# A fused diffusion step: the first norm with features on the partitions instead of transposing x on the chip

## The chip, the cores and the metric

The kernel runs on one core of one Trainium2 chip. The metric is the device time of one execution in microseconds (us). The kernel before takes 1057.17 us, the median of three runs (1056.76 to 1060.57).

## The reference, cut to what matters

One trunk layer works on 640 tokens of width 1024: 512 latent tokens and 128 context tokens. The change lies in its first step, the norm with modulation ahead of the big input projection:

```
h = rmsnorm(x, pre1) * (1 + scale1) + shift1        # shift1, scale1: from silu(c) @ w_ada + b_ada
mq, mk, mv, mo, mg, cq, ckv, krope, merge = split(h @ w_in)
```

rmsnorm divides each token by the root of the mean of its 1024 squares; scale and shift have one value per feature, and differ between latent and context tokens. After this come a bidirectional mLSTM, an attention, a merge and an MLP of width 4096, which the change does not touch.

## The kernel before, in words

Activations that feed a projection are kept with the features on the 128 partitions: h1h and h1l, 8 blocks of 128 features by 640 tokens, are the high and the low part of h, and every product is three float32r matmuls (high by high, high by low, low by high).

The head of the kernel (L175 to L232) makes h. x is read as five tiles of 128 tokens by 1024 features (L185 to L188). Per tile ACT squares and sums it along the free axis (L194), `rstd_of` takes the mean on DVE (L98) and the power -1/2 on POOL (L100), and DVE scales the tile by it (L196). Two blocks of the query weights are loaded meanwhile; `load_w` casts them to the high part on ACT (L111) and takes the low part on POOL here (L112).

`features(k)` then works on block k of 128 features. It issues the load of block k+1 of the modulation weights (aw, 1 MB each, L181, six buffers). `ada_rows` multiplies block k of those weights with silu(c) in eight plain float32 matmuls (L149) and copies the sums out (L150). `ada_cols` transposes them (L155) and adds up four partial sums (L157, L158); two small DVE instructions make the factor A and the offset B (L206, L207). Five transposes on TensorE (L210, L211) bring the x block into PSUM with features on the partitions. ACT and DVE each apply A and B (L215 writes h1h, L216 a float32 copy), once for the 512 latent and once for the 128 context tokens, and DVE takes the low part as the difference (L217).

The loop at L222 calls `features(k + 1)` and then issues the twelve query matmuls of block k (L229). Right behind it come the p1 products (L269 onwards), whose weights partly reuse the buffers of the query weights.

The order in which an engine issues its instructions is not that of the source: a planner goes through the program with its own model of times and puts the instructions of each engine in the order in which it finds them ready. All loads of the head are issued from SP's queue.

Of the kernel before, what the change touches and what calls it, by code (L numbers as in the profile page):

```python
# [6 lines left out]
F32 = mybir.dt.float32  # L7
# [19 lines left out]
def _build(ctx, tc, nc, a, dbg):  # L27
# [44 lines left out]
    def bank2():  # L72
        return psum[2][1].tile([P, 1024], F32, name="b2")
# [21 lines left out]
    def rstd_of(ss, n, width, name):  # L95

        ms = small.tile([P, 8], F32, name="ms")[:, 0:n]
        V.tensor_scalar(out=ms, in0=ss, scalar1=1.0 / width, scalar2=EPS, op0=ALU.mult, op1=ALU.add)  # L98
        r = small.tile([P, 8], F32, name="rs_" + name)[:, 0:n]
        G.tensor_tensor(out=r, in0=ms, in1=mhalf[:, 0:n], op=ALU.pow)  # L100
        return r

    def load_w(src, eng=V):

        n = src.shape[1]
        raw = pW_.tile([P, 1024], F32, name="raw", bufs=2)[:, 0:n]
# [23 lines left out]
    def halves(ps):  # L130
        return ps.rearrange("p (h n) -> p h n", h=2)
# [41 lines left out]
        S.activation(out=qT[:, j, :].rearrange("p (h n) -> p h n", h=2), in_=ps[:, :, 0:320], func=AF.Copy, scale=128.0 ** -0.5)  # L173

    with pool("pX", side="right") as pX:  # L175
        xt = []
        aw = []

        def ada_load(f):
            w = pX.tile([P, KD, 256], F32, name="aw", bufs=6)  # L180
            nc.sync.dma_start(w, a["w_ada1"][f].rearrange("p (k n) -> p k n", k=KD))  # L181
            aw.append(w)
        ada_load(0)
        nc.sync.dma_start(cst[:, 0:128], a["consts"][:, 0:128])
        for t in range(NT):  # L185
            x = pX.tile([P, 1024], F32, name=f"x{t}")
            nc.sync.dma_start(x, a["x"][t])
            xt.append(x)  # L188
        wq = [[x.rearrange("p (k n) -> p k n", k=8) for x in load_w(a["w_q"][j], G)] for j in range(2)]
        qps = [halves(bank2()) for j in range(2)]  # L190
        for t in range(NT):
            sq = pX.tile([P, 1024], F32, name="sq", bufs=1)
            ss = small.tile([P, 1], F32, name="ss")
            S.activation(out=sq, in_=xt[t], func=AF.Square, accum_out=ss)  # L194
            r = rstd_of(ss, 1, 1024, "x")
            V.tensor_scalar(out=xt[t], in0=xt[t], scalar1=r, scalar2=None, op0=ALU.mult)  # L196

        def features(k):
            if k + 1 < KD:
                ada_load(k + 1)  # L200
            rows = pX.tile([P, 256], F32, name="ar", bufs=2)
            ada_rows([aw[k][:, i, :] for i in range(KD)], 256, rows)
            pc = bank1()
            m = ada_cols(rows, 2, pc[:, 128:384].rearrange("p (b x) -> p b x", b=2), 2 * k, "1")
            A, B = modA[0][:, k, :], modB[0][:, k, :]
            V.tensor_scalar(out=A, in0=m[:, 0, :], scalar1=1.0, scalar2=pre1[:, k:k + 1], op0=ALU.add, op1=ALU.mult)  # L206
            V.tensor_copy(B, m[:, 1, :])  # L207
            px = bank1()
            for t in range(4):
                T.transpose(px[:, t * 128:(t + 1) * 128], xt[t][:, k * 128:(k + 1) * 128], ident)  # L210
            T.transpose(pc[:, 0:128], xt[4][:, k * 128:(k + 1) * 128], ident)  # L211

            tmp = pX.tile([P, TOK], F32, name="tmp", bufs=3)
            for ps, c, i in ((px, slice(0, 512), 1), (pc[:, 0:128], slice(512, 640), 0)):
                S.activation(out=h1h[:, k, c], in_=ps, func=AF.Identity, scale=A[:, i:i + 1], bias=B[:, i:i + 1])  # L215
                V.tensor_scalar(out=tmp[:, c], in0=ps, scalar1=A[:, i:i + 1], scalar2=B[:, i:i + 1], op0=ALU.mult, op1=ALU.add)  # L216
            V.tensor_tensor(out=h1l[:, k, :], in0=tmp, in1=h1h[:, k, :], op=ALU.subtract)  # L217

        features(0)
        nc.sync.dma_start(cst[:, 128:640], a["consts"][:, 128:640])  # L220
        nc.sync.dma_start(hvec, a["hvec"])
        for k in range(KD):  # L222
            if k + 1 < KD:
                features(k + 1)
            for u, v in ((0, h1h), (1, h1h), (0, h1l)):
                for j in range(2):
                    for hf in range(2):
                        c = slice(hf * 320, hf * 320 + 320)
                        T.matmul(qps[j][:, hf, 0:320], wq[j][u][:, k, :], v[:, k, c], start=k == 0 and u == 0 and v is h1h,  # L229
                                 stop=k == KD - 1 and v is h1l)  # L230
        for j in range(2):
            q_evac(j, qps[j])  # L232
# [933 lines left out]
def prepare(i):  # L1166
    import numpy as np
    c_ = np.ascontiguousarray
    cols = lambda v: c_(v.reshape(-1, 128).T)
    d = {}  # L1170
    d["x"] = c_(np.concatenate([i["x_sample"][0], i["x_prompt"][0]], 0).reshape(5, 128, 1024))
    d["cache_ckv"] = c_(i["cache_mla_ckv"][0, 0])
    d["cache_krope"] = c_(i["cache_mla_krope"][0, 0])
    cn = i["state_mlstm_C"][0, 0].transpose(0, 2, 1, 3)
    nn = i["state_mlstm_n"][0, 0].transpose(0, 2, 1)[..., None]
    d["state"] = c_(np.concatenate([cn, nn], -1))
    cv = np.stack([i["c_ctx"], i["c"][0]], -1)
    cv = cv.reshape(8, 128, 2).transpose(1, 0, 2).reshape(128, 16)
    wa = i["w_ada"][0].reshape(1024, 6, 8, 128)
    d["w_ada1"] = _piece_a(wa[:, [1, 0]].transpose(0, 2, 1, 3).reshape(1024, 2048), 8, 256)  # L1180
    d["w_ada2"] = _piece_a(wa[:, [4, 3, 2, 5]].reshape(1024, 4096), 2, 512)
    b = i["b_ada"][0].reshape(6, 8, 128)
    b = np.concatenate([b[[1, 0]].transpose(1, 0, 2).reshape(16, 128), b[[4, 3, 2, 5]].reshape(32, 128)], 0).reshape(-1)
    d["vecs"] = c_(np.concatenate([cols(i["norm_pre1"][0]), cols(i["norm_pre2"][0]), c_(i["mlstm_head_norm"][0].T), cols(b),
                                   cols(i["norm_post1"][0]), cols(i["norm_post2"][0]), cv], 1))
    gb = i["mlstm_gate_b"][0]
    d["hvec"] = c_(np.stack([gb[:, 0].reshape(8), gb[:, 1].reshape(8), i["state_mlstm_m"][0, 0].reshape(8)], 1))
    d["kv_norm"], d["q_norm"] = c_(i["mla_kv_norm"][0]), c_(i["mla_q_norm"][0])
    w = i["w_in"][0]
    d["w_q"], d["w_k"] = _piece_b(w[:, 0:512]), _piece_b(w[:, 512:1024])  # L1190
    d["w_v"], d["w_o"] = _piece_a(w[:, 1024:1536], 2, 512), _piece_b(w[:, 1536:2048])
    d["w_p1"] = _piece_a(np.concatenate([w[:, 2048:2064], w[:, 2448:2704], w[:, 2704:2736]], 1), 2, 304)
    d["w_cq"] = _piece_a(w[:, 2064:2448], 2, 384)
    d["w_g"] = _piece_b(w[:, 2736:4784])
    d["w_uq"] = _piece_a(i["w_uq"][0].reshape(384, 768), 1, 768)
    ukv = i["w_ukv"][0]
    d["w_uk"] = c_(_piece_b(ukv[:, :, 0:64].reshape(256, 512)).transpose(1, 0, 2).reshape(128, 1024))
    d["w_uv"] = _piece_a(ukv[:, :, 64:128].reshape(256, 512), 2, 512)[0]
    d["w_y"] = c_(np.concatenate([_piece_b(i["w_mlstm_o"][0]), _piece_b(i["w_mla_o"][0])], 2))
    d["w_out"] = _piece_a(i["w_out"][0], 2, 512)  # L1200
    d["w_mlp1"] = _piece_b(i["w_mlp1"][0])
# [45 lines left out]
```

## Time and profile before

| what | value |
|---|---|
| median of three runs | 1057.17 us (1056.76 to 1060.57) |
| the profiled execution, its own time | 1055.42 us |
| its span, first to last instruction | 1053.7 us |
| TensorE (PE) busy | 1022.7 us, 97% of the span |
| VectorE (DVE) busy | 561.0 us |
| ScalarE (ACT) busy | 424.2 us |
| GpSimd (POOL) busy | 238.1 us |
| read from HBM | 105.03 MB |

Busy time is that of one engine's instructions; PE stands for the matmuls and PEld for the loads of their stationary side, which overlap them. The chain that ended last is followed back from the last instruction to what released each one. Times within the span count from its start.

### The profile page before, as it was taken

The page shows a single profiled execution, that of the slowest core. Times are in us where ns is not written, and L with a number is a line of the kernel's source. Part 1 is how long each engine was busy: PE and PEld are TensorE (multiplying, and loading weights), DVE is VectorE, ACT ScalarE, POOL GpSimd, SP SyncE. Part 2 cuts the span into 40 slices and gives each one's busy share as a digit, 9 for nine tenths or more (in the row PEclk, how much of TensorE's full clock was granted, in tenths as well). Part 3 has the DMA queues.
Part 4 walks back from the last instruction along what each step waited for, and adds up shares of the span by engine and source line. Part 5 has one row for each costly group of instructions (what it writes and reads, how often), then busy time and mean ns, then how long its engine had stood idle before and what let it go on. Part 6 is the DMA issues. An engine that isn't in the chain of part 4 may idle for free.

```text
span 1053.7 us, 15728 instructions
## 1 busy us (share of the span) xinstructions
PE 1022.7 (97%) x6342; PEld 907.0 (86%) x6342; DVE 561.0 (53%) x955; ACT 424.2 (40%) x784; POOL 238.1 (23%) x218
## 2 busy tenths in 40 slices
PE   4999999899999999999999998999999999999997
PEld 2899899888889888888888897898989898989896
DVE  4655255767664222222334489365566565656557
ACT  4354244277775222222223564442425152515142
POOL 3011225424560000001000015224040404040101
PEclk9999999999999999999999999999999999999999
DMA  9444132211002444444446251231313131313034
GB/s 372 168 129 145 46 109 73 75 41 41 15 8 79 139 143 140 141 140 141 140 141 223 77 180 62 79 121 40 120 40 120 40 120 41 121 41 121 1 111 169
DMA packets 40121, 112.03 MB, mean 106 GB/s; under 512 B 4280, under 2 KB 14168, under 8 KB 38768
## 3 DMA queue, kind: packets, MB, share of 16 engines
q1 hardware_dynamic: 34656, 92.92, 25.8%
q0 software_dynamic: 4672, 16.80, 4.9%
q10 hardware_dynamic: 720, 1.31, 0.3%
q8 instruction: 50, 0.82, 0.3%
q14 instruction: 23, 0.19, 0.1%
HBM read 105.03 MB, written 5.98 MB: 105 GB/s over the span
## 4 chain that ended last, share of the span: by engine, by line
PE 89%; DVE 5%; ACT 2%; issue 2%; DMA 1%; POOL 1%; SPq 0%; POOLq 0%; DVEq 0%; ACTq 0%
PE b L116 20%; PE b L117 20%; PE b L118 20%; PE b L937 7%; PE bY L937 5%; PE b L149 3%; PE bV L937 2%; PE bW L937 2%; PE b L695 2%; PE b L683 2%; PE b L229 1%; PE b L496 1%; PE b L470 1%; DMA x<-x 1%; DMA gate<-w_mlp 1%
## 5 line engine op out<-in xcount | busy, mean ns | idle before, releaser
L112 DVE TENSOR_TENSOR wl<-raw,wh 128x1024 fp32r<-128x1024 f32 (+2 forms) x67 | 80.5, 1202 | 157.7 <-ACT wh L111 156.4
L111 ACT CAST wh<-raw 128x1024 fp32r<-128x1024 f32 (+2 forms) x69 | 69.8, 1013 | 175.0 <-PE b L117 157.0
L117 PE MATMUL b<-h1l,wh 128*128 128x320 f32 x400 | 125.2, 313 | 0.0
L116 PE MATMUL b<-h1h,wh 128*128 128x320 f32 x384 | 119.9, 312 | 0.0
L118 PE MATMUL b<-h1h,wl 128*128 128x320 f32 x384 | 118.9, 310 | 0.0
L117 PEld LDWEIGHTS b<-h1l,wh 128*128 128x128 f32 x400 | 75.2, 188 | 6.9 <-issue 6.9
L116 PEld LDWEIGHTS b<-h1h,wh 128*128 128x128 f32 x384 | 72.2, 188 | 7.1 <-DVE sg L808 5.0
L845 POOL TENSOR_TENSOR x<-gate 128x512 f32<-128x512 f32 x14 | 19.7, 1406 | 235.2 <-DMA gate<-w_mlp 220.8
L118 PEld LDWEIGHTS b<-h1h,wl 128*128 128x128 f32 x384 | 72.2, 188 | 0.3 <-issue 0.2
L117 PE MATMUL b<-wlx,uh 128*128 128x512 f32 (+1 forms) x164 | 64.5, 393 | 2.4 <-DVE wlx L112 2.4
L116 PE MATMUL b<-whx,uh 128*128 128x512 f32 (+1 forms) x164 | 64.1, 395 | 1.6 <-ACT u L995 1.6
L1125 DVE TENSOR_TENSOR h1h<-h1h,b 128x512 f32<-128x512 f32 (+1 forms) x71 | 46.2, 673 | 35.8 <-PE b L118 35.6
L117 PE MATMUL b<-wl,uh 128*128 128x512 f32 x160 | 63.2, 395 | 0.0
L116 PE MATMUL b<-wh,uh 128*128 128x512 f32 x160 | 62.1, 396 | 0.0
L118 PE MATMUL b<-whx,ul 128*128 128x512 f32 (+1 forms) x164 | 61.5, 393 | 0.0
L118 PE MATMUL b<-wh,ul 128*128 128x512 f32 x160 | 60.4, 394 | 0.0
L742 POOL DMA_DIRECT2D aw<-w_ada x32 | 17.4, 545 | 185.8 <-PE b L149 178.6
L999 ACT CAST uh<-u 128x320 fp32r<-128x320 f32 x64 | 29.3, 459 | 74.4 <-DVE u L996 48.7
L612 POOL TENSOR_TENSOR pt<-pt,sm 128x640 f32<-128x640 f32 x32 | 40.0, 1255 | 46.7 <-DVE sm L610 44.5
L112 DVE TENSOR_TENSOR wlx<-raw,whx 128x1024 fp32r<-128x1024 f32 (+2 forms) x28 | 34.6, 1234 | 27.9 <-ACT whx L111 27.8
L149 PE MATMUL b<-aw,csil 128*32 128x256 f32 (+1 forms) x256 | 35.2, 519 | 6.4 <-DMA aw<-w_ada 6.4
L117 PEld LDWEIGHTS b<-wlx,uh 128*128 128x128 f32 x164 | 31.1, 190 | 9.6 <-DVE wlx L112 2.8
(432 smaller groups left out, 2812.8 us busy)
## 6 DMA issues: line engine op xcount, KB each, us to landing
raw<-w_mlp SPq DMA_DIRECT2D x36, 512.0 KB, 3.2
aw<-w_ada POOLq DMA_DIRECT2D x32, 512.0 KB, 4.2
gate<-w_mlp SPq DMA_DIRECT2D x28, 512.0 KB
aw<-w_ada SPq DMA_DIRECT2D x8, 1024.0 KB, 12.0
raw<-w_g SPq DMA_DIRECT2D x16, 512.0 KB, 5.3
x<-x SPq DMA_DIRECT2D x10, 512.0 KB, 8.0
raw<-w_y SPq DMA_DIRECT2D x8, 512.0 KB, 3.3
raw<-w_out SPq DMA_DIRECT2D x8, 512.0 KB, 4.3
```

The source lines that it names most:

```text
L111: S.copy(hi, raw)
L112: eng.tensor_tensor(out=lo, in0=raw, in1=hi, op=ALU.subtract)
L116: T.matmul(out, lh, rh, start=start, stop=False)
L117: T.matmul(out, lh, rl, start=False, stop=False)
L118: T.matmul(out, ll, rh, start=False, stop=stop)
L149: T.matmul(ps[32 * j:32 * j + 32, 0:n], csil[:, k, :], raws[k], start=k < 4, stop=k >= 4, tile_position=(0, 32 * j))
L612: G.tensor_tensor(out=pt, in0=pt, in1=sm.broadcast_to([P, 640]), op=ALU.mult)
L683: T.transpose(pp[:, j * 128:(j + 1) * 128], pt[:, j * 128:(j + 1) * 128], ident)
L695: T.matmul(pv[64 * e:64 * e + 64, 0:128], vn[:, j, h * 64:(h + 1) * 64], pT[:, j, e * 128:e * 128 + 128], start=j == 0, stop=j == 4, tile_ ...
L937: T.matmul(out, w[u][:, k, :], x[v][:, k, :], start=start and k == 0 and i == 0, stop=k == 3 and i == 2, skip_group_check=True)
L999: S.copy(uh[:, c], u)
L1125: V.tensor_tensor(out=o, in0=o, in1=ps, op=ALU.add)
```

## The change

x is read a second time over in another layout: the host also hands in xT, 8 blocks of 128 features by 640 tokens, and the head reads that (eight loads of 320 KB in place of five of 512 KB; x itself is still read later on for the residual). The transposes of x are gone. Since the features now lie on the partitions, the sum of squares runs across partitions: ACT squares each block, DVE adds the eight results, five small float32 matmuls with a matrix of ones add across the partitions and put the tokens on the partitions, `rstd_of` works on all 640 tokens at once, DVE spreads the result on the diagonals of five 128 by 128 matrices, and two matmuls with ones as the stationary side copy it to all partitions (rb). In `features(k)` x is multiplied in place by rb, on DVE for block 0 and on POOL for the others; ACT and DVE read x from SBUF where they read the transposed x from PSUM. The modulation is split off as `mod(k)`, which is issued one block further ahead, and the loads of the query weights stand behind the norm in the source.

```diff
+        nc.sync.dma_start(cst[:, 0:128], a["consts"][:, 0:128])
         ada_load(0)
-        nc.sync.dma_start(cst[:, 0:128], a["consts"][:, 0:128])
-        for t in range(NT):
-            x = pX.tile([P, 1024], F32, name=f"x{t}")
-            nc.sync.dma_start(x, a["x"][t])
-            xt.append(x)
-        wq = [[... for x in load_w(a["w_q"][j], G)] for j in range(2)]
-        for t in range(NT):
-            S.activation(out=sq, in_=xt[t], func=AF.Square, accum_out=ss)
-            r = rstd_of(ss, 1, 1024, "x")
-            V.tensor_scalar(out=xt[t], in0=xt[t], scalar1=r, scalar2=None, op0=ALU.mult)
+        xt = pX.tile([P, KD, TOK], F32, name="xt")
+        for k in range(KD):
+            nc.sync.dma_start(xt[:, k, :], a["xT"][k])
-        def features(k):
+        def mod(k):
             if k + 1 < KD:
                 ada_load(k + 1)
...
-            px = bank1()
-            for t in range(4):
-                T.transpose(px[:, t * 128:(t + 1) * 128], xt[t][:, k * 128:(k + 1) * 128], ident)
-            T.transpose(pc[:, 0:128], xt[4][:, k * 128:(k + 1) * 128], ident)
+            mods[k] = A, B
+        def features(k):
+            if k + 1 < KD:
+                mod(k + 1)
+            A, B = mods[k]
+            x = xt[:, k, :]
+            (V if k == 0 else G).tensor_tensor(out=x, in0=x, in1=rb, op=ALU.mult)
...
-                S.activation(out=h1h[:, k, c], in_=ps, func=AF.Identity, ...)
-                V.tensor_scalar(out=tmp[:, c], in0=ps, ...)
+                S.activation(out=h1h[:, k, c], in_=x[:, c], func=AF.Identity, ...)
+                V.tensor_scalar(out=tmp[:, c], in0=x[:, c], ...)
             V.tensor_tensor(out=h1l[:, k, :], in0=tmp, in1=h1h[:, k, :], op=ALU.subtract)
+        mod(0)
+        for k in range(KD):
+            sq = acc if k == 0 else pX.tile([P, TOK], F32, name="sq", bufs=2)
+            S.activation(out=sq, in_=xt[:, k, :], func=AF.Square)
+            if k:
+                V.tensor_tensor(out=acc, in0=acc, in1=sq, op=ALU.add)
+        for t in range(NT):
+            T.matmul(pss[:, t, :], acc[:, t * 128:(t + 1) * 128], ones[:, 0:8], start=True, stop=True)
+        r = rstd_of(pss[:, :, 0], NT, 1024, "x")
+        V.tensor_tensor(out=diag, in0=ident.unsqueeze(1).broadcast_to([P, NT, 128]), in1=r.unsqueeze(2).broadcast_to([P, NT, 128]),
+                        op=ALU.mult)
+        for hf in range(2):
+            c = slice(hf * 320, hf * 320 + 320)
+            ps = bank1()[:, 0:320]
+            T.matmul(ps, ones, diag.rearrange("p t n -> p (t n)")[:, c], start=True, stop=True)
+            (V.tensor_copy if hf else S.copy)(rb[:, c], ps)
+        wq = [[... for x in load_w(a["w_q"][j], G)] for j in range(2)]
...
+    d["xT"] = c_(d["x"].reshape(640, 8, 128).transpose(1, 2, 0))
```

## Rows read from the trace of the kernel before

**Rows 1.** The page: busy time by engine, and the chain that ended last.
```profile
PE 1022.7 (97%) x6342; PEld 907.0 (86%) x6342; DVE 561.0 (53%) x955; ACT 424.2 (40%) x784; POOL 238.1 (23%) x218
...
PE 89%; DVE 5%; ACT 2%; issue 2%; DMA 1%; POOL 1%; SPq 0%; POOLq 0%; DVEq 0%; ACTq 0%
```

**Rows 2.** Windows: length, PE, PEld, DVE, ACT, POOL busy, granted clock, DMA share, GB/s.
```profile
6.40:21.10 14.70, 6.85 (x29) 3.33 (x29) 8.79 (x17) 9.15 (x15) 7.80 (x7) 1.00 1.03 417
21.10:24.30 3.20, 3.20 (x29) 2.14 (x28) 0.77 (x3) 0.37 (x1) 0.00 (x0) 1.00 1.02 425
24.30:46.00 21.70, 21.70 (x207) 17.01 (x207) 16.05 (x46) 10.01 (x20) 1.30 (x3) 1.00 0.64 238
46.00:60.00 14.00, 14.00 (x102) 14.00 (x101) 3.87 (x9) 3.72 (x6) 0.13 (x1) 1.00 0.26 77
```

**Rows 3.** Timeline from 12 to 23 us: start, length, instruction, idle before and releaser.
```profile
12.96 1.06 ACT L194 ACTIVATE sq<-x 128x1024 f32<-128x1024 f32 x1 [0.15 <-DMA x<-x]
...
15.80 5.11 POOL L112 TENSOR_TENSOR wl<-raw,wh 128x1024 fp32r<-128x1024 f32 x2
15.86 2.83 DVE L196 TENSOR_SCALAR x<-x,rs_x 128x1024 f32<-128x1024 f32 x1 [0.72 <-POOL rs_x L100]
...
18.88 1.79 PE L229 MATMUL b<-h1h,wh 128*128 128x320 f32 x4
...
21.13 1.52 PE L149 MATMUL b<-aw,csil 128*32 128x256 f32 x16
```

**Rows 4.** The chain in order of time, one step of the loop over blocks.
```profile
31.43 1.00 PE b L149 x16
32.69 0.88 PE b L229 x6
33.78 0.44 PE b L210 x4
34.22 0.88 PE b L229 x6
```

**Rows 5.** View of line L149, first 10 us, then whole span: ns min/median/max.
```profile
L149 PE MATMUL b<-aw,csil x16: 604/634/636, 6.4 to 7.7; 128*32 128x256 f32 x16
...
L149 PE MATMUL b<-aw,csil x128: 379/379/636, 6.4 to 43.1; 128*32 128x256 f32 x128
```

**Rows 6.** Timeline at 131 us: plain float32 matmuls, two instructions for each.
```profile
131.77 1.06 PE L451 MATMUL b<-qT,kT 128*128 128x128 f32 x8
```

**Rows 7.** Groups by line and shape, 0 to 50 us: busy us, mean ns, idle.
```profile
L196 DVE TENSOR_SCALAR x<-x,rs_x 128x1024 f32<-128x1024 f32 x5 | 5.8, 1168 | 3.0 <-POOL rs_x L100 3.0
L100 POOL TENSOR_TENSOR rs_x<-ms,mhalf 128x1 f32<-128x1 f32 x5 | 2.7, 543 | 12.3 <-DVE ms L98 12.3
...
L98 DVE TENSOR_SCALAR ms<-ss 128x1 f32<-128x1 f32 x5 | 0.7, 148 | 5.9 <-ACT sq L194 5.9
```

**Rows 8.** Groups by line and shape, whole span.
```profile
L1024 DVE COPY z<-b 128x320 f32<-128x320 f32 x14 | 6.8, 485 | 1.9 <-PE b L937 1.9
...
L853 ACT CAST mix<-gate 128x512 fp32r<-128x512 f32 x14 | 8.7, 620 | 22.1 <-DMA gate<-w_mlp 18.4 <-PE bW L937 2.5 <-DVE S6l L979 1.3
...
L978 ACT CAST S3h<-h1h 128x640 fp32r<-128x640 f32 x4 | 2.8, 727 | 0.0
```

**Rows 9.** Views of lines L217 and L1062: ns min/median/max, first and last start.
```profile
L217 DVE TENSOR_TENSOR h1l<-tmp,h1h x8: 815/820/1398, 20.2 to 49.2; 128x640 fp32r<-128x640 f32 x8
...
L1062 POOL TENSOR_TENSOR h1h<-h1h x2: 1567/3464/5360, 630.0 to 635.3; 128x640 f32<-128x640 f32 x2
```

**Rows 10.** Timeline at 636 us: POOL and DVE at work side by side.
```profile
636.83 4.27 POOL L1059 TENSOR_TENSOR mix<-mix,h1h 128x640 f32<-128x640 f32 x2
...
639.58 2.20 DVE L1065 TENSOR_TENSOR h1h<-h1h,mix 128x640 f32<-128x640 f32 x1
```

**Rows 11.** DMA issues, 0 to 50 us, and a wait of SP's queue.
```profile
aw<-w_ada SPq DMA_DIRECT2D x8, 1024.0 KB, 12.0
x<-x SPq DMA_DIRECT2D x5, 512.0 KB, 8.0
...
SPq L181 <- DMA x<-x: 2.8, 3, 0.9
```

More of the change, by code (lines that the diff above doesn't have):

```diff
@@ L175, in _build @@
     with pool("pX", side="right") as pX:
-        xt = []
         aw = []
@@ L182, in ada_load @@
             aw.append(w)
+        nc.sync.dma_start(cst[:, 0:128], a["consts"][:, 0:128])
         ada_load(0)
-        nc.sync.dma_start(cst[:, 0:128], a["consts"][:, 0:128])
-        for t in range(NT):
-            x = pX.tile([P, 1024], F32, name=f"x{t}")
-            nc.sync.dma_start(x, a["x"][t])
-            xt.append(x)
-        wq = [[x.rearrange("p (k n) -> p k n", k=8) for x in load_w(a["w_q"][j], G)] for j in range(2)]
-        qps = [halves(bank2()) for j in range(2)]
-        for t in range(NT):
-            sq = pX.tile([P, 1024], F32, name="sq", bufs=1)
-            ss = small.tile([P, 1], F32, name="ss")
-            S.activation(out=sq, in_=xt[t], func=AF.Square, accum_out=ss)
-            r = rstd_of(ss, 1, 1024, "x")
-            V.tensor_scalar(out=xt[t], in0=xt[t], scalar1=r, scalar2=None, op0=ALU.mult)
-        def features(k):
+        xt = pX.tile([P, KD, TOK], F32, name="xt")
+        for k in range(KD):
+            nc.sync.dma_start(xt[:, k, :], a["xT"][k])
+        mods = {}
+        def mod(k):
             if k + 1 < KD:
@@ L203, in features @@
             pc = bank1()
-            m = ada_cols(rows, 2, pc[:, 128:384].rearrange("p (b x) -> p b x", b=2), 2 * k, "1")
+            m = ada_cols(rows, 2, pc[:, 0:256].rearrange("p (b x) -> p b x", b=2), 2 * k, "1")
             A, B = modA[0][:, k, :], modB[0][:, k, :]
@@ L213, in features @@
             tmp = pX.tile([P, TOK], F32, name="tmp", bufs=3)
-            for ps, c, i in ((px, slice(0, 512), 1), (pc[:, 0:128], slice(512, 640), 0)):
-                S.activation(out=h1h[:, k, c], in_=ps, func=AF.Identity, scale=A[:, i:i + 1], bias=B[:, i:i + 1])
-                V.tensor_scalar(out=tmp[:, c], in0=ps, scalar1=A[:, i:i + 1], scalar2=B[:, i:i + 1], op0=ALU.mult, op1=ALU.add)
+            for c, i in ((slice(0, 512), 1), (slice(512, 640), 0)):
+                S.activation(out=h1h[:, k, c], in_=x[:, c], func=AF.Identity, scale=A[:, i:i + 1], bias=B[:, i:i + 1])
+                V.tensor_scalar(out=tmp[:, c], in0=x[:, c], scalar1=A[:, i:i + 1], scalar2=B[:, i:i + 1], op0=ALU.mult, op1=ALU.add)
@@ L217, in features @@
             V.tensor_tensor(out=h1l[:, k, :], in0=tmp, in1=h1h[:, k, :], op=ALU.subtract)
+        mod(0)
+        ones = const.tile([P, 128], F32, name="ones")
+        G.memset(ones, 1.0)
+        acc = pX.tile([P, TOK], F32, name="sqa")
+        for k in range(KD):
[3 more added lines that the diff above has]
+                V.tensor_tensor(out=acc, in0=acc, in1=sq, op=ALU.add)
@@ new lines, in _build @@
+        pss = bank1()[:, 0:8 * NT].rearrange("p (t x) -> p t x", x=8)
+        for t in range(NT):
+            T.matmul(pss[:, t, :], acc[:, t * 128:(t + 1) * 128], ones[:, 0:8], start=True, stop=True)
+        r = rstd_of(pss[:, :, 0], NT, 1024, "x")
+        diag = pX.tile([P, NT, 128], F32, name="diag")
+        V.tensor_tensor(out=diag, in0=ident.unsqueeze(1).broadcast_to([P, NT, 128]), in1=r.unsqueeze(2).broadcast_to([P, NT, 128]),
+                        op=ALU.mult)
+        rb = pX.tile([P, TOK], F32, name="rb")
@@ L219, in _build @@
+        for hf in range(2):
[3 more added lines that the diff above has]
+            (V.tensor_copy if hf else S.copy)(rb[:, c], ps)
+        wq = [[x.rearrange("p (k n) -> p k n", k=8) for x in load_w(a["w_q"][j], G)] for j in range(2)]
+        qps = [halves(bank2()) for j in range(2)]
         features(0)
```

## The prediction, made before the changed kernel was run

> **What bounds the kernel now.** The page comes first: PE is busy for 1022.7 us of the 1053.7 us span, and the chain that ended last runs over PE for 89% [rows 1]. So what a change in the head is worth is what it does to PE: work taken from it, or a start moved. The windows say where PE idles: from 6.4 to 21.1 us it is busy for 6.85 of 14.7 us, and from 21.1 to 60 us it has no gap at all [rows 2]. So the head has two parts. Up to 21.1 us PE waits for the norm of x; the timeline shows the chain, from the last x tile (ACT starts on it at 12.96) over the scaling on DVE at 15.86 to the first query matmul at 18.88 [rows 3]. After 21.1 us PE sets the pace: a us of its work removed there is a us gained, and a us by which that stretch starts later is a us lost. The chain of waits shows what a loop step is made of: 16 modulation instructions 1.00 us, twice six query matmuls 0.88 us each, four transposes of x 0.44 us [rows 4].
>
> **Removed.** 40 transposes. The five of block 0 ran in PE's idle time and are worth nothing. For seven blocks L210 costs 0.44 us each [rows 4]. L211 lies between 32.43, where the modulation ends, and 32.69, where the matmuls go on; it gets 0.11 us (a quarter of L210's 0.44) to all of the 0.26 us. That is 7 x 0.55 = 3.9 to 7 x 0.70 = 4.9 us; I take 4.2, since that pause can hardly all be L211's. The five scalings on DVE (L196, 5.8 us [rows 7]) leave the chain, but they were waited for only ahead of 18.88.
>
> **Added ahead of the first query matmul.** The order is a new chain that can't start before all of x is there, where before a tile at a time went through.
> - Loads. The bytes are the same 2.6 MB, and the DMA engines are full in this stretch at 417 GB/s [rows 2], so I leave the last block at 12.9 us [rows 3]. Eight issues replace five on SP; SP already runs so far ahead that it waits for landings (three waits, 2.8 us [rows 11]), so three issues more cost nothing as long as it does. Moved: the identity's load ahead of aw, one issue; the query weights' loads behind the second aw megabyte, 2.5 us at that rate. They are wanted only when block 0 is ready, some 7 us later, and that is their cover; the modulation loads behind them keep their place in bytes.
> - Squares, 0.73 us a block (L978, same shape [rows 8]), keep step with the loads (0.32 MB, 0.8 us). The adds on DVE at 0.82 us [rows 9] do so barely: seven are 5.7 us, and four small instructions of mod(0) at 0.15 (L98 [rows 7]) go between, 0.6 us. The first add can start at about 8.8, so the sum is ready at 15.1; at best 0.73 + 0.82 behind the last block, 14.5.
> - Five matmuls with ones are ten instructions. The near row is 8 in 1.06 us [rows 6], 0.13 each: 1.3 us. In the head the same matmul took 634 ns where it takes 379 later, a factor 1.67 [rows 5], although the granted clock reads 1.00, which is the 2.4 GHz level, in every window [rows 2]: 2.2 us. I take 2.0, nearer the head's row: 17.1.
> - Mean and power, 0.15 + 0.54 [rows 7], on PE's result: 17.9. The diagonals on DVE, 0.82 [rows 9]: 18.7.
> - Two matmuls of 320 columns. By [rows 6] scaled with columns, 4 x 0.33 = 1.3 us, times 1.67 = 2.2 in the head. I take 2.0: 20.7. The second half's copy 0.49 [rows 8]: 21.2. x times rb for block 0 on DVE 0.82, and 1.40 if POOL is at work [rows 9]: 22.0 to 22.6. The activation, 0.62 from SBUF (L853 [rows 8]): 23.1. Some eight hand-offs between engines at about 0.1 us, an estimate from the gaps of the chain [rows 4]: 24.0.
>
> So the unbroken stretch starts at 24.0 where it started at 21.1: **+2.9 us**. With all short values it is 21.2. At the long end the power waits on POOL behind the two subtractions for the query weights, 5.11 us [rows 3]: 27 to 30.
>
> **Moved into the idle time.** Modulation blocks 1 and 2 no longer stand behind block 0's query matmuls. PE can do them between 15 and 24 us, when their weights land (2.5 us apart). Each takes 1.00 for L149 and 0.21 for its transposes, the rest of the gap between 32.69 + 0.88 and 33.78 [rows 4]: **-2.4 us**; three blocks -3.6, if the planner runs that far ahead.
>
> **Still to be done.** Six query matmuls of block 0 lay ahead of 21.1 us, 0.88 us [rows 4]: **+0.9**. The stretch before began with about 0.6 us of slow matmuls (L149 1.52 where it takes about 1.0 later [rows 3, 4]); the one after begins with 0 to 2 us more, by how broken PE's work is up to there; I take 1.2, net **+0.6**.
>
> **Lying beside PE.** In the loop POOL multiplies seven blocks by rb, 1.57 us each at the least [rows 9]; DVE's pass goes from PSUM to SBUF, ACT's too. If nothing collides, that stays under the 3.0 us that PE needs for a step (3.68 less the transposes), and POOL can run ahead, as all of x is there.
>
> **Sum:** 2.9 - 4.2 - 2.4 + 0.9 + 0.6 = -2.2 us; with the third modulation block in the idle time as likely as not, -2.7. Against the profiled execution's own 1055.42 us that is 1052.7; its time lies 1.75 below the median of the runs, so against that **1054.5 us**. Short ends everywhere: 0.1 - 4.9 - 3.6 + 0.9 - 0.6 = -8.1, 1049.1. The power behind both subtractions, start at 30, no third block: 8.9 - 3.9 - 2.4 + 0.9 + 0.6 = +4.1, 1061.3.
>
> **Rivals.**
> 1. *The idle time is used in full:* short start, three modulation blocks early. For it: PE idles 7.85 us there, and the planner orders by readiness. Against: those instructions ran slow in the head, and the sum of squares is serial. -6 to -8 us: 1049 to 1051. Chance 0.22.
> 2. *The norm queues on POOL:* the power behind the subtractions. For it: both are wanted at 17 to 18 us. Against: before, all five powers went first. Start at 27.5 to 30, +1.5 to +4: 1059 to 1061. Chance 0.11.
> 3. *POOL and DVE get in each other's way in the loop, and the loop goes slower than before.* Rows show it: a scaling, 0.75 us in the four others ((5.8 - 2.83) / 4 [rows 7]), took 2.83 us while POOL subtracted [rows 3], L217 took 1.40 instead of 0.82 [rows 9], and side by side POOL's 640-wide multiply took 2.14 and DVE's 2.20 [rows 10]. If each of POOL's multiplies and both big DVE passes of a step run at such prices one behind the other, 2.14 + 2.20 + 0.4 (half of that scaling, for 512 columns), the step is 4.7 us, against 3.68 before. Block 7's low part was begun at 49.2 [rows 9]; it would be at 24 + 7 x 4.7 = 57, so +6 to +8: 1063 to 1065. It decides from 3.68 us a step on. Against it: in [rows 10] the two alternate, so 2.14 already holds the other's wait, and counting no wait twice gives 1.57 + 0.82 + 0.4 = 2.8 us, under PE's 3.0. Chance 0.10.
>
> The Trainium skill, "SBUF — State Buffer", section "Who interferes with whom", says that such a DVE instruction (two SBUF inputs, or a two-port mode) and a POOL instruction reading SBUF hold a shared port pair for the whole instruction, and the later one fully blocks. The 2.83 us in [rows 3] agree: it ends 0.33 us after the first of POOL's two, at 15.80 + 5.11 / 2. By that rule the loop's port time is the sum without double counting, so it speaks for the 2.8 us, and against putting this multiply on POOL with little to spare.
>
> That the transposes stay is no rival: nothing else would issue them.
>
> **How the numbers follow.** The forecast, 0 to -5 us, has 0.57. About 0.5% (5.3 us) is what a measurement of this kernel can tell from no change: below 1051.9 or above 1062.5. Faster gets rival 1 and a little of the forecast's edge, 0.24; slower rival 3 and the far end of 2, 0.11; the rest, 0.65, is the same. The range runs from rival 1's middle, 1049.5, to rival 2's end, 1061; it leaves out most of rival 3 and the very short end.
>
> **What would show it.** Right: no transposes of x; first query matmul at 23 to 25 us; two or three blocks of L149's matmuls ahead of it; then PE without a gap, at about 3 us a step. Wrong: a first query matmul before 22 or after 27; gaps of PE in the loop that end on POOL's multiply or DVE's subtraction (rival 3); the power waiting behind L112 on POOL (rival 2); or a shift after 60 us that the head doesn't have, since the planner may order the rest anew.

## The result, and the profile after

The changed kernel takes 1068.55 us (median of six runs, 1066.03 to 1069.09), against 1057.61 for the kernel before on the same chip (six runs, 1055.65 to 1061.43). The ratio is 1.0093, with a 95% interval of 1.0071 to 1.0115: slower by more than the 0.5% that counts here, and above the range. The profiled execution has a span of 1064.2 us, against 1053.7 before. Times read from a trace, here and below, come from one profiled execution of each kernel, which lies up to 2.5 us from the median of that kernel's runs.

The page of the changed kernel: busy time by engine, and the chain that ended last.

```profile
PE 1024.4 (96%) x6316; PEld 908.2 (85%) x6316; DVE 567.1 (53%) x956; ACT 424.8 (40%) x783; POOL 248.5 (23%) x222
...
PE 85%; DVE 7%; DMA 2%; ACT 2%; issue 2%; POOL 1%; SPq 0%; DVEq 0%; POOLq 0%; ACTq 0%
```

Beside [rows 1] the totals hardly move: PE is busy 1.7 us longer, though its transposes of x are gone, and idle for 39.8 us of its span instead of 31.0. The shares of the chain (PE 85% instead of 89%, DVE 7% instead of 5%) look like an answer and are none: the chain of e1 below has the same 85% and 7% in a kernel 9 us faster, and that of e4, the slowest kernel of all, has 89% and 5%. The windows of the changed kernel (length, PE, PEld, DVE, ACT, POOL busy, granted clock, DMA share, GB/s) say more; the first two are windows of [rows 2], too.

```profile
6.40:21.10 14.70, 4.90 (x28) 3.19 (x28) 7.70 (x13) 8.14 (x11) 2.71 (x2) 1.00 1.04 415
...
24.30:46.00 21.70, 16.24 (x122) 10.63 (x124) 18.70 (x28) 7.24 (x15) 12.60 (x8) 0.84 0.50 202
...
30.00:33.00 3.00, 1.08 (x9) 0.59 (x4) 2.96 (x3) 0.00 (x0) 3.00 (x2) 1.00 1.04 401
33.00:36.00 3.00, 0.21 (x1) 0.21 (x2) 2.86 (x4) 1.07 (x2) 3.00 (x3) 0.53 0.62 257
36.00:39.00 3.00, 3.00 (x14) 2.49 (x18) 2.90 (x4) 0.38 (x2) 1.92 (x2) 0.50 0.02 5
```

The stretch from 24.3 to 46 us had no gap on PE before. Now PE is busy for 16.24 of its 21.70 us, and POOL, which did 1.30 us there, does 12.60. The last three windows show the hole itself: from 30 to 36 us PE works for 1.29 of 6 us, while DVE and POOL are busy throughout. PE's granted clock falls within the hole: it reads 1.00 from 30 to 33 us, in which PE works for 1.08 us, then 0.53, and 0.50, the 1.2 GHz level, from 36 to 39 us. The first matmuls behind the hole run at that clock.

One line serves as a landmark for what the head costs. The gate sums are the first products behind the query and p1 products that the head feeds. Their line, in the kernel before and then in the changed one (count, ns min/median/max, first and last start):

```profile
L298 PE MATMUL b<-cst,LgF x10: 272/273/303, 65.4 to 72.0; 128*40 128x128 f32 x10
```

```profile
L320 PE MATMUL b<-cst,LgF x10: 272/273/303, 74.9 to 80.2; 128*40 128x128 f32 x10
```

They start 9.5 us later. The spans differ by 10.5 us, so in these two executions nine tenths of the loss lies ahead of this point. The timeline of the changed kernel shows how it comes about (start, length, engine, line, instruction, and in brackets the idle time before it and what ended that):

```profile
15.76 2.27 PE L227 MATMUL b<-ones,sqa 128*128 128x8 f32 x10 [5.58 <-DVE sqa L224]
18.39 1.19 POOL L100 TENSOR_TENSOR rs_x<-ms,mhalf 128x5 f32<-128x5 f32 x1 [17.40 <-DVE ms L98]
19.53 5.24 POOL L112 TENSOR_TENSOR wl<-raw,wh 128x1024 fp32r<-128x1024 f32 x2
19.61 2.95 DVE L230 TENSOR_TENSOR diag<-cst,rs_x 128x640 f32<-128x640 f32 x1 [1.38 <-POOL rs_x L100]
22.62 2.50 PE L236 MATMUL b<-diag,ones 128*128 128x320 f32 x4 [4.59 <-DVE diag L230]
25.05 1.68 PE L149 MATMUL b<-aw,csil 128*32 128x256 f32 x16
25.79 12.13 POOL L207 TENSOR_TENSOR xt<-xt,rb 128x640 f32<-128x640 f32 x7 [1.03 <-DVE rb L237]
26.60 3.14 DVE L212 TENSOR_SCALAR tmp<-xt,modA,modB 128x512 f32<-128x512 f32 x2
27.47 0.95 PE L251 MATMUL b<-h1h,wh 128*128 128x320 f32 x4 [0.74 <-ACT h1h L211]
29.85 1.99 DVE L213 TENSOR_TENSOR h1l<-tmp,h1h 128x640 fp32r<-128x640 f32 x1
31.89 0.85 PE L251 MATMUL b<-h1l,wh 128*128 128x320 f32 x4 [1.67 <-DVE h1l L213]
31.96 1.31 DVE L158 TENSOR_TENSOR mc<-mc,vecs 128x4 f32<-128x4 f32 x1
33.30 1.46 DVE L198 TENSOR_SCALAR modA<-mc,vecs 128x2 f32<-128x2 f32 x1
34.94 3.07 DVE L212 TENSOR_SCALAR tmp<-xt,modA,modB 128x512 f32<-128x512 f32 x2
35.79 1.44 PE L251 MATMUL b<-h1h,wh 128*128 128x320 f32 x4 [3.04 <-ACT h1h L211]
```

Two runs of POOL stand in it, and DVE stretches beside each. Beside the two subtractions for the query weights (19.53 to 24.77) the diagonals take 2.95 us. Then POOL makes all seven multiplications by rb in one go, 25.79 to 37.92, because all of x lies ready and each product goes back into its own place: POOL waits for no buffer. In that time every DVE instruction of the list is long, even one on 4 and one on 2 elements a partition (1.31 and 1.46 us). PE waits first for block 0's low part, then for block 1: its activation needs the factor A, which DVE finishes at 34.76.

### The profile page after: what moved, and what is told of

It is laid out like the page before. It is cut to its first block, busy times and chain, and to the rows that moved or that the text cites. A ratio compares the mean times of both kernels' runs of the same rounds, so it can differ in the third digit from the quotient of the medians.

```text
span 1064.2 us, 15704 instructions
## 1 busy us (share of the span) xinstructions
PE 1024.4 (96%) x6316; PEld 908.2 (85%) x6316; DVE 567.1 (53%) x956; ACT 424.8 (40%) x783; POOL 248.5 (23%) x222
## 3 DMA queue, kind: packets, MB, share of 16 engines
q10 hardware_dynamic: 720, 1.31, 0.3%
## 4 chain that ended last, share of the span: by engine, by line
PE 85%; DVE 7%; DMA 2%; ACT 2%; issue 2%; POOL 1%; SPq 0%; DVEq 0%; POOLq 0%; ACTq 0%
PE b L116 19%; PE b L118 19%; PE b L117 19%; PE b L959 7%; PE bY L959 5%; PE b L149 3%; PE bV L959 2%; PE bW L959 2%; PE b L717 2%; PE b L251 1%; PE b L705 1%; PE b L492 1%; DMA raw<-w_mlp 1%; DVE wl L112 1%; PE b L494 1%
## 5 line engine op out<-in xcount | busy, mean ns | idle before, releaser
L1147 DVE TENSOR_TENSOR h1h<-h1h,b 128x512 f32<-128x512 f32 (+1 forms) x71 | 46.2, 673 | 38.7 <-PE b L118 38.6
L149 PE MATMUL b<-aw,csil 128*32 128x256 f32 (+1 forms) x256 | 36.0, 533 | 6.9 <-DMA aw<-w_ada 6.9
```

The costliest lines, as they stand in the source:

```text
L149: T.matmul(ps[32 * j:32 * j + 32, 0:n], csil[:, k, :], raws[k], start=k < 4, stop=k >= 4, tile_position=(0, 32 * j))
L1147: V.tensor_tensor(out=o, in0=o, in1=ps, op=ALU.add)
```

## The experiments

**Theory and rivals.** The theory after this reading: POOL's unbroken run of multiplications holds up DVE, PE starves behind DVE, and the cost lies in blocks 0 and 1. Rivals: the norm's longer chain ahead of the first query matmul is what costs; or the gain expected from modulation done early is missing. Each is changed by itself below. All edits are to the changed kernel unless another is named, and the ratio is always to the kernel before, run on the same chip.

**e1: no multiplications but block 0's.**

```diff
-            (V if k == 0 else G).tensor_tensor(out=x, in0=x, in1=rb, op=ALU.mult)
+            if k == 0:
+                V.tensor_tensor(out=x, in0=x, in1=rb, op=ALU.mult)
```

> Left out: the multiplication of blocks 1 to 7 by rb (block 0 keeps it), so POOL has no multiplications at all and h is wrong for seven blocks. Theory 'port' (seven multiplications in one run on POOL, 25.8 to 37.9 us, each hold DVE's two-input and fast instructions back, so blocks 0 and 1 are late and TensorE idles): DVE's instructions return to their lone times (L212 about 0.4, L213 0.83, L158 0.16), TensorE's gaps between 28 and 36 us go, the clock stays at 1.00, and the last query matmul, 61.8 us in the changed kernel, comes 7 to 9 us earlier; time about 1060, level with before. Rival 'start' (the first query matmul at 27.5 in place of 18.9 us is the loss, what follows is covered): the last query matmul moves by less than 2 us, time 1066 to 1068. Rival 'order' (the planner's new order after 60 us is the loss): as 'start'.

Measured: 1059.27 us, ratio 1.0019 (1.0006 to 1.0032). The first query matmul starts at 27.6, as late as in the changed kernel (27.5); the gate sums start at 68.4 instead of 74.9. The trace of e1, its timeline, then the window from 27 to 60 us (the changed kernel, then e1), then e1's line of the gate sums:

```profile
26.75 0.80 DVE L213 TENSOR_SCALAR tmp<-xt,modA,modB 128x512 f32<-128x512 f32 x2
27.98 0.83 DVE L214 TENSOR_TENSOR h1l<-tmp,h1h 128x640 fp32r<-128x640 f32 x1 [0.43 <-ACT h1h L212]
29.61 0.16 DVE L158 TENSOR_TENSOR mc<-mc,vecs 128x4 f32<-128x4 f32 x1
29.81 0.23 DVE L198 TENSOR_SCALAR modA<-mc,vecs 128x2 f32<-128x2 f32 x1
```

```profile
27.00:60.00 33.00, 27.82 (x221) 21.64 (x222) 26.28 (x56) 12.21 (x25) 12.68 (x11) 0.90 0.36 132
27.00:60.00 33.00, 32.39 (x267) 26.90 (x268) 20.04 (x58) 14.84 (x29) 1.69 (x4) 1.00 0.39 140
```

```profile
L321 PE MATMUL b<-cst,LgF x10: 272/272/303, 68.4 to 73.7; 128*40 128x128 f32 x10
```

The same DVE instructions that took 3.14 (a pair), 1.99, 1.31 and 1.46 us take 0.80, 0.83, 0.16 and 0.23. PE has no gap from its first query matmul on (the missing 0.61 us is the time from 27 to 27.61), and the clock reads 1.00. So the multiplications cost 6.5 us at the gate sums, two thirds of the loss. They don't make up all of it: 3.0 us against the kernel before remain. The 6.5 us have two parts. PE is idle for 5.2 us of this window in the changed kernel and for 0.6 in e1: 4.6 us. And behind the hole, from 35.79 to 40.28 us, the changed kernel does in 4.49 us, at the lower clock, the block of work that e1 does in 2.69 (31.01 to 33.70): 1.8 us.

**e2: the multiplications on DVE.**

```diff
-            (V if k == 0 else G).tensor_tensor(out=x, in0=x, in1=rb, op=ALU.mult)
+            V.tensor_tensor(out=x, in0=x, in1=rb, op=ALU.mult)
```

> All eight multiplications on DVE, nothing left out. Theory 'port': DVE gets 7 x 0.83 = 5.8 us more work but waits for nobody; a step is 0.83 + 0.8 + 0.83 + 0.7 = 3.2 us on DVE against 3.2 to 3.5 on TensorE, so gaps of TensorE are short; the last query matmul comes 4 to 7 us earlier, time about 1062 to 1064. 'start' and 'order': DVE becomes the slower engine, no gain or a loss, 1068 to 1072.

Measured: 1061.29 us, ratio 1.0031 (1.0014 to 1.0047); gate sums at 69.9. The trace of e2, one line of its timeline:

```profile
25.67 5.97 DVE L207 TENSOR_TENSOR xt<-xt,rb 128x640 f32<-128x640 f32 x8
```

5 of the 6.5 us come back, so it is the engine that the multiplications run on, and not the work, that costs. The remaining 1.5 us have the same root on another engine: all eight were ready at once, the planner put them in one row, and block 0's low part waits behind seven multiplications that nobody wants yet; it is done at 33.3 us.

**e7 and e8: the multiplications held back.** The product goes to a ring of two buffers, so that the third waits until block 0 is used up; on POOL in e7, as shown, and on DVE in e8 (V in place of the bracket).

```diff
-            (V if k == 0 else G).tensor_tensor(out=x, in0=x, in1=rb, op=ALU.mult)
+            xn = pX.tile([P, TOK], F32, name="sq", bufs=2)
+            (V if k == 0 else G).tensor_tensor(out=xn, in0=x, in1=rb, op=ALU.mult)
+            x = xn
```

> The changed kernel, with the multiplications still on POOL, but out of place into a ring of two tiles, so that block k+2 can't be multiplied before block k has been read. It tells 'seven in one run' from 'on POOL at all'. If the run is the cost: DVE's blocked time falls from about 8 us to 2 or 3 in the stretch from 25 to 38 us, the gate sums come at 70 to 72 us, time 1063 to 1065. If POOL at all is the cost (each multiplication holds DVE back once, whenever it is done): the same seven waits, spread out, gate sums at 74 to 76, time 1067 to 1069.

> As the run with all multiplications on DVE (1061.3 us), but out of place into a ring of two. There the planner issued all eight in one row of 5.97 us, ahead of block 0's own copy, and TensorE idled for some 3 us. Expected: two in a row at the most, block 0's low part 3 to 4 us earlier, gate sums at 67 to 68 us in place of 69.9, time 1058 to 1060. If DVE's sum of work is the bound, no change: 1061.

Measured: e7 1064.44 us, ratio 1.0071 (1.0056 to 1.0086), gate sums at 73.2. e8 1060.5 us, 1.0039 (1.0025 to 1.0053), gate sums at 68.8, a little later than expected. The trace of e7, the line of the multiplication (ns min/median/max), then two windows:

```profile
L208 POOL TENSOR_TENSOR sq<-xt,rb x7: 2109/2172/3035, 26.2 to 48.7; 128x640 f32<-128x640 f32 x7
```

```profile
36.00:46.00 10.00, 9.24 (x84) 6.24 (x84) 8.56 (x23) 5.44 (x12) 5.51 (x3) 1.00 0.28 78
46.00:60.00 14.00, 12.17 (x93) 10.98 (x92) 9.41 (x20) 3.98 (x8) 5.38 (x6) 1.00 0.11 26
```

At the gate sums e8 is only 0.4 us behind e1, which has no multiplications, and 1.1 us ahead of e2: by this landmark, most of what e2 lost was their order. The times don't confirm a gain of that size: e8's ratio lies above e2's, and the intervals overlap. e7 lies between the two readings and settles less. Spread over the loop, POOL's multiplication takes 2.17 us instead of 1.73, a step takes about 3.9 us, and only 1.7 us of the 6.5 come back. So the run ahead is the worse form, but the collision remains at this pace, too: the two windows show gaps of 2.6 us on PE, and the longest, 1.83 us, ends at 52.41 with block 6, whose factors DVE finishes late. Not all of the 4.8 us that are left are such gaps. About 1.5 us lie in the first matmuls: from 27.87 to 32.09 they take 4.22 us for what takes 2.69 in e1 (27.61 to 30.30), though the granted clock reads 1.00. How DVE's waits and POOL's divide was not separated.

**e11: POOL busy, but only writing.** In place of each multiplication of blocks 1 to 7 POOL fills a tile that nobody reads any more, three times.

```diff
-            (V if k == 0 else G).tensor_tensor(out=x, in0=x, in1=rb, op=ALU.mult)
+            if k == 0:
+                V.tensor_tensor(out=x, in0=x, in1=rb, op=ALU.mult)
+            else:
+                for _ in range(3):
+                    G.memset(diag, 0.0)
```

> Left out: the multiplication of blocks 1 to 7. In the place of each, POOL fills a dead tile of 128x640 with zeros three times (21 fills of about 0.63 us, 13 us in one run, as long as the seven multiplications), so POOL is as busy but reads nothing from SBUF. If any work on POOL holds DVE back: blocks 0 and 1 as late as in the changed kernel, gate sums at 74 to 75, time 1066 to 1069. If it takes POOL's reads to hold DVE's second input back: L213 and L158 run at their lone 0.83 and 0.16 us beside the fills, and only L212 (one tensor input, a scaled copy) can still be held; gate sums at 68.5 to 71, time 1059.5 to 1062.

Measured: 1061.54 us, ratio 1.0042 (1.0024 to 1.006); gate sums at 70.0. The trace of e11, its timeline:

```profile
25.62 15.06 POOL L211 MEMSET diag<- 128x640 f32 x21 [0.42 <-PE b L240]
...
27.04 1.52 DVE L216 TENSOR_SCALAR tmp<-xt,modA,modB 128x512 f32<-128x512 f32 x2
28.67 0.83 DVE L217 TENSOR_TENSOR h1l<-tmp,h1h 128x640 fp32r<-128x640 f32 x1
30.38 0.16 DVE L158 TENSOR_TENSOR mc<-mc,vecs 128x4 f32<-128x4 f32 x1
30.58 0.68 DVE L198 TENSOR_SCALAR modA<-mc,vecs 128x2 f32<-128x2 f32 x1
```

POOL is busy here for longer than with the multiplications, 15.06 against 12.13 us, and the gate sums lose 1.6 us to e1 instead of 6.5. The two DVE instructions with two inputs from SBUF take just what they take in e1, 0.83 and 0.16; those with one input are still held, by 0.7 us for the pair and by 0.45. So a busy POOL is not the cost by itself: the DVE instructions with two inputs waited for a POOL that reads SBUF, and for one that only writes they did not. For those with one input the run says less, because a fill takes 0.72 us where a multiplication takes 1.73; how far their shorter waits come from that was not separated.

**e3: the low part of the query weights on DVE,** so that POOL is idle while the norm is made.

```diff
-        wq = [[... for x in load_w(a["w_q"][j], G)] for j in range(2)]
+        wq = [[... for x in load_w(a["w_q"][j])] for j in range(2)]
```

> The two subtractions for the query weights go from POOL to DVE. Every theory: the diagonals on DVE (2.95 us in the changed kernel) take 0.83, unless the planner puts a subtraction of 1.2 us ahead of them; POOL's multiplications start right after rb. 'port': the run of seven on POOL stays, so the gain is only the 1 to 2 us of the start; first query matmul at 25.5 to 26.5, time 1066 to 1067.5. 'start': what is gained at the start is gained at the end, too, but no more than 2 us either.

Measured: 1064.16 us, somewhat faster than expected, ratio 1.006 (1.0041 to 1.0078). The trace of e3, the line of the diagonals:

```profile
L230 DVE TENSOR_TENSOR diag<-cst,rs_x x1: 824/824/824, 19.9 to 19.9; 128x640 f32<-128x640 f32 x1
```

The diagonals fall from 2.95 to 0.82 us, and the first query matmul comes at 25.6 instead of 27.5. Of these 1.9 us, 1.3 arrive at the gate sums (73.6), where blocks 0 and 1 are still held by the multiplications.

**e4: the modulation of block 1 ahead of the norm.**

```diff
-            if k + 1 < KD:
+            if k + 1 < KD and k + 1 not in mods:
                 mod(k + 1)
...
         mod(0)
+        mod(1)
```

> mod(1) is called right after mod(0), ahead of the norm; nothing else is moved. In the changed kernel TensorE issues its instructions in order, and those of mod(1) stood behind the two matmuls with ones, at 25.05 us, though the weights had landed. Expected: they run at 16 to 19 us, and DVE's L158 and L198 of block 1 (1.31 and 1.46 us within POOL's run) are out of that run. 'port': block 1 is ready some 2 to 3 us earlier, and TensorE has 1.2 us less to do behind the start; time 1065 to 1067. 'start': 1.2 us at the most, 1067 to 1068.

Measured: 1070.32 us, ratio 1.0113 (1.0087 to 1.0138); gate sums at 78.2, first query matmul at 32.3. A miss, and worth reading. The trace of e4, its timeline:

```profile
16.01 1.93 PE L149 MATMUL b<-aw,csil 128*32 128x256 f32 x16 [5.74 <-DMA aw<-w_ada]
18.91 2.14 PE L228 MATMUL b<-ones,sqa 128*128 128x8 f32 x10
20.89 2.34 POOL L112 TENSOR_TENSOR wl<-raw,wh 128x1024 fp32r<-128x1024 f32 x1 [19.90 <-ACT wh L111]
23.19 1.19 POOL L100 TENSOR_TENSOR rs_x<-ms,mhalf 128x5 f32<-128x5 f32 x1
24.41 2.95 DVE L231 TENSOR_TENSOR diag<-cst,rs_x 128x640 f32<-128x640 f32 x1 [3.15 <-POOL rs_x L100]
```

On PE the matmuls with ones, ready at about 15.8, now come behind the modulation of block 1 and its transposes, and the modulation waits for its weights until 16.01: they start at 18.91. That shift of 3 us puts the power behind POOL's first subtraction and the diagonals beside the second: the prediction's rival 2, which the changed kernel just escaped (there the subtractions start as the power ends).

**e5: no multiplication of its own.** DVE makes x times A times rb in one instruction, ACT adds B, and DVE makes the low part as (tmp + B) - h1h, also in one; POOL has no part in it. The query weights as in e3, and the modulation of block 1 between the matmuls with ones and the rest of the norm.

```diff
-            (V if k == 0 else G).tensor_tensor(out=x, in0=x, in1=rb, op=ALU.mult)
...
+                V.scalar_tensor_tensor(out=tmp[:, c], in0=x[:, c], scalar=A[:, i:i + 1], in1=rb[:, c], op0=ALU.mult, op1=ALU.mult)
+                S.activation(out=h1h[:, k, c], in_=tmp[:, c], func=AF.Identity, scale=1.0, bias=B[:, i:i + 1])
+                V.scalar_tensor_tensor(out=h1l[:, k, c], in0=tmp[:, c], scalar=B[:, i:i + 1], in1=h1h[:, k, c], op0=ALU.add, op1=ALU.subtract)
...
+        mod(1)
         r = rstd_of(pss[:, :, 0], NT, 1024, "x")
...
+        wq = [[... for x in load_w(a["w_q"][j])] for j in range(2)]
```

> Nothing left out. Three edits: x times A times rb is one DVE instruction and the part with B another, so the multiplication is no pass of its own and POOL has none; the subtractions for the query weights go to DVE; mod(1) is called between the five matmuls with ones and the rest of the norm. Theory 'port' (POOL's work beside DVE is the loss; the rest is a start some us late): POOL holds nothing back, the first query matmul starts at 24 to 25 us, TensorE has no gap after it, a step is 3.1 to 3.4 us, and the gate sums (74.9 us in the changed kernel, 65.4 before) come at 63 to 66: time 1054 to 1058, level with before or a little faster. Theory 'start' (a chain that needs all of x before anything can be done costs more than the transposes did): the gate sums stay later than 67, time above 1059.

Measured: 1054.06 us over ten runs (1053.26 to 1057.44), ratio 0.9978 (0.9967 to 0.9989): **faster than both kernels**, though by less than the 0.5%. The gate sums start at 63.4, 2.0 us ahead of the kernel before. The trace of e5, its windows (columns as in [rows 2]) and then its timeline:

```profile
6.40:21.10 14.70, 7.46 (x47) 4.47 (x48) 7.03 (x13) 7.17 (x11) 1.19 (x1) 1.00 1.03 412
...
24.30:46.00 21.70, 21.20 (x194) 17.15 (x187) 19.46 (x58) 11.18 (x24) 1.28 (x3) 1.00 0.65 243
```

```profile
17.98 1.94 PE L149 MATMUL b<-aw,csil 128*32 128x256 f32 x16
19.63 0.82 DVE L229 TENSOR_TENSOR diag<-cst,rs_x 128x640 f32<-128x640 f32 x1 [1.38 <-POOL rs_x L100]
24.81 1.93 DVE L209 SCALAR_TENSOR_TENSOR tmp<-xt,modA,rb 128x512 f32<-128x512 f32 x4
```

The hole is gone (21.20 of 21.70 us, POOL 1.28), and PE has modulation to do at 17.98 while POOL and DVE make the norm.

**e9, e10, e12: which part of e5 does it.** e12 is the fused form alone; e9 adds the query weights on DVE, e10 the early modulation.

```diff
 e9, from e5:
-        mod(1)
 e10, from e5:
-        wq = [[... for x in load_w(a["w_q"][j])] for j in range(2)]
+        wq = [[... for x in load_w(a["w_q"][j], G)] for j in range(2)]
 e12: both
```

> The two-pass kernel (1054.1 us) with mod(1) back in its old place, behind the whole norm in the source; nothing else changed. If TensorE's idle time between the two groups of matmuls with ones is worth what it holds: L149 of block 1 runs behind the second group again, 1.2 to 1.9 us of work more behind the start, gate sums at 64.5 to 66 in place of 63.4, time 1055 to 1057. If the idle time is worth nothing (the start is set by DVE's chain alone): no change.

> The two-pass kernel with the subtractions for the query weights back on POOL; mod(1) stays between the groups. It prices POOL's two subtractions, 5.2 us, when no multiplications stand behind them. 'port': they hold back whichever of DVE's two-input instructions comes with them (the diagonals or the first pass over block 0, up to 2.2 us), gate sums at 64 to 66, time 1055 to 1057. If DVE has slack there: 63 to 64, 1054.

> The changed kernel with the two-pass form alone: no multiplication of its own on POOL or elsewhere, the query weights' subtractions still on POOL, mod(1) still behind the norm. It completes the square with the three two-pass runs (both edits 63.4 us at the gate sums, weights on DVE alone 65.6, mod(1) early alone 67.5). If the edits add up: 65.6 + 67.5 - 63.4 = 69.7 us, time about 1060.5. If POOL's two subtractions cost more or less without the early mod(1) (there they stood beside DVE's instructions for mod(1); here they stand beside the diagonals, 2.95 us in the changed kernel): 68 to 71.

| kernel | weights' low part | modulation 1 | first query matmul | gate sums | time, us | ratio (95%) |
|---|---|---|---|---|---|---|
| e12 | POOL | late | 27.2 | 68.1 | 1058.88 | 1.0009 (0.9997 to 1.0021) |
| e9 | DVE | late | 25.0 | 65.6 | 1056.53 | 0.9996 (0.9986 to 1.0006) |
| e10 | POOL | early | 27.6 | 67.5 | 1058.67 | 1.0017 (1.0007 to 1.0027) |
| e5 | DVE | early | 26.4 | 63.4 | 1054.06 | 0.9978 (0.9967 to 0.9989) |

The fused form alone brings 6.8 of the 9.5 us back. Taking POOL off the weights brings 2.5 us, the early modulation 0.6, and both together 4.7: 1.6 more than the two added. The 0.6 us don't show in the times of e12 and e10, whose intervals overlap, and e10 came later than expected (64 to 66). Its trace shows why the modulation is worth little while POOL subtracts, the timeline and one window:

```profile
21.54 4.66 POOL L112 TENSOR_TENSOR wl<-raw,wh 128x1024 fp32r<-128x1024 f32 x2 [1.78 <-ACT wh L111]
21.70 2.22 DVE L198 TENSOR_SCALAR modA<-mc,vecs 128x2 f32<-128x2 f32 x1
24.46 3.46 DVE L209 SCALAR_TENSOR_TENSOR tmp<-xt,modA,rb 128x512 f32<-128x512 f32 x4
27.55 1.05 PE L250 MATMUL b<-h1h,wh 128*128 128x320 f32 x4 [2.54 <-ACT h1h L210]
```

```profile
28.00:36.00 8.00, 8.00 (x62) 5.61 (x62) 5.68 (x18) 2.61 (x7) 0.00 (x0) 0.79 0.86 346
```

The subtractions come later there and hold block 1's factor A (2.22 us) and block 0's pass (3.46, against 1.93 in e5). PE idles for 2.54 us ahead of its first query matmul, and then its granted clock reads 0.79 from 28 to 36 us, where e12's reads 1.00. An estimate of what that costs is 8 x 0.21 = 1.7 us, as much as the 1.6 above; so the extra gain of the two edits together may be that the clock stays up. e5 also shows that the first query matmul alone is a poor measure: it comes 1.4 us later than in e9, and the gate sums 2.2 us sooner, because three blocks of modulation lie ahead of it.

**e6: the kernel before, with the query weights' low part on DVE.** It asks whether the collision in [rows 3] had a price of its own.

> The kernel BEFORE, with one edit: the two subtractions for the query weights go from POOL to DVE. 'port': the last scaling of x, 2.83 us in the kernel before, takes 0.75, the first query matmul comes 1 to 2 us earlier (17 to 18 us), and the time falls by 1 to 2 us, to about 1056. Against it: DVE gets 2.4 us of subtractions, which may stand ahead of the modulated copies, and nothing or 1 us is lost.

Measured: 1058.5 us, ratio 1.0007 (0.9997 to 1.0017): no gain. The trace of e6, its timeline:

```profile
15.85 0.75 DVE L196 TENSOR_SCALAR x<-x,rs_x 128x1024 f32<-128x1024 f32 x1 [0.72 <-POOL rs_x L100]
19.65 0.90 PE L229 MATMUL b<-h1h,wl 128*128 128x320 f32 x2 [0.45 <-DVE wl L112]
20.48 1.94 PE L149 MATMUL b<-aw,csil 128*32 128x256 f32 x16
```

The last scaling takes 0.75 instead of 2.83 us, and the first query matmul starts at 16.8 instead of 18.9. But then PE waits for the weights' low part, which DVE now makes in turn, and its matmuls run slow: 1.94 us for what took 1.52 in [rows 3]. The gate sums start at 66.1, against 65.4.

## Why the prediction was wrong

At the gate sums the forecast stood at 65.4 - 2.7 = 62.7 us; 74.9 was measured. With e1 the 12.2 us that are missing divide as follows (the stretch is taken to start with the first query matmul):

| step of the sum | forecast | measured | missing |
|---|---|---|---|
| start of the unbroken stretch | 24.0 | 27.6 (e1) | 3.6 |
| its length without multiplications in the way | 38.7 | 40.8 (e1: 27.6 to 68.4) | 2.1 |
| multiplications on POOL | 0 | 6.5 (74.9 - 68.4) | 6.5 |

**"Lying beside PE"** is the step that failed. The right mechanism stood in the text as rival 3, with a chance of 0.10 and a price by the step (1063 to 1065 us, still below the measured 1068.55), and was held unlikely because 2.8 us of port time a step fit under PE's 3.0. That count was a mean over the loop. The trace of after shows no such mean: "POOL can run ahead, as all of x is there" was written as a relief and is the harm. All seven multiplications fall on blocks 0 and 1, PE has no other work yet to cover them, and DVE has some five waits of up to a whole multiplication each, about 8 us by the rows of after and e1: (3.14 - 0.80) + (1.99 - 0.83) + (1.31 - 0.16) + (1.46 - 0.23) + (3.07 - 0.81). The last pair, one 512-wide and one 128-wide instruction, takes the 0.81 in e1's second block. Its place was wrong as well: two late blocks, not a longer step eight times over. The slow clock behind the hole, 0.50 where it read 1.00 in every window of [rows 2], was in no term; it makes up about 1.8 of the 6.5 us. The prediction's [rows 10] are subtractions by the source, not the multiplies it calls them, but their price of 2.14 us carried over: e7's multiplications took 2.17.

The Trainium skill's rule weighed in the prediction ("SBUF — State Buffer", "Who interferes with whom") holds in these runs; it was the use made of it that failed. It says that the pair is held for the whole instruction, and 1.31 us for a 0.16 us instruction agree. It also says that two SBUF inputs contend only with a GpSimd instruction that reads SBUF, while copies and tensor_scalar in a two-port mode contend with any, and e11 agrees in both halves: 0.83 and 0.16 unheld, 1.52 and 0.68 held. Whether those one-input instructions ran in such a mode the trace does not show.

**The start,** forecast by the chain of the norm. The sum of squares was done at 15.6 (15.1 forecast) and the matmuls with ones took 2.27 us (2.0): right in kind. The power took 1.19 us on 128x5, where 0.54 had been carried over from 128x1 [rows 7]; a term mis-sized by 0.65. The diagonals took 2.95 instead of 0.82: rival 2's place, but not its form. The power did not queue behind POOL's subtractions; it went first, and the subtractions started at 19.53, just ahead of the diagonals on DVE. e3 puts 1.9 us at the first query matmul on this. The prediction had costed block 0's multiplication with and without such a collision, and the diagonals without. The hand-offs between engines, put at 0.1 us each although [rows 4] shows no such gap, took 0.03 to 0.15 in this chain: that term was about right, though not by the rows that it names.

**Modulation in idle time.** Two blocks and half a third were counted, ahead of the first query matmul; one block came (25.05). The second and the half third are 1.7 of the 2.1 us in the second line. The idle time was there, but in the source the modulation stands behind the norm's matmuls, and on PE it came behind them (L236 at 22.62). e5 puts block 1 between the norm's two sets of matmuls and has three blocks ahead of the first query matmul; e4 shows that the place matters more than the idea.

**Right** were the transposes, gone, with a loop that has no gap once nothing is in the way (e1), and the loads: the first matmul of the norm did not wait longer than the sum on DVE allows. The range missed because its upper end was rival 2, and rival 3, the only one beyond it, was given too small a chance and a price judged by a mean.

## What to carry over

Port time that fits under the bound on average still costs where one engine may run ahead: ask when its instructions will be issued, not only how many there are a step. At the gate sums, putting them on the engine that would otherwise wait brought back 5 of 6.5 us here, and holding them back on POOL 1.7. An operation moved off a path is best folded into an instruction that has to run anyway: here a second factor in a pass over the same data cost less than a separate pass on an engine that was idle (e12 against the changed kernel). Early work for PE pays only where PE's order lets it in; placed ahead of something that is ready sooner, it delays it.

## What was not expected of the hardware

- DVE instructions of 2 and 4 elements a partition were held for most of a POOL instruction: L198 1.46 us instead of 0.23, L158 1.31 instead of 0.16, and in e10 L198 2.22 beside a subtraction. Measured by their own length, small instructions in a chain are hit hardest.
- SCALAR_TENSOR_TENSOR is held too: 3.46 us beside POOL, 1.93 without, for four.
- An earlier start can be worth nothing: in e6 PE began 2.1 us sooner in a broken stretch and ran its matmuls slow (1.94 us for L149's sixteen where a step of the loop takes 1.00 [rows 4]) while the granted clock read 1.00. The first matmuls of e7 ran slow, too, at the same reading (1.44 us for L149's sixteen at 30.72). What slows them no run here tells apart.
- From the gate sums to the end the kernels take 987.8 to 992.2 us in their profiles (before 988.3, after 989.3), though no edit touches the code there. Runs of one kernel differ by 2 to 6 us. Much of the spread seems to lie in which run was profiled: this part is longest in e11 and e10 (992.2 and 991.7), whose profiled runs lie 2.5 and 2.4 us above their medians, and shortest in e12 and e8 (987.8 and 987.9), whose runs lie 1.3 and 2.0 below. That the order of the rest moved is not shown.
